# Zero rows in the memory cell's small products, and an early operation on ScalarE

## The chip, the cores and the metric

One core of a Trainium2 chip runs the whole program in one launch. The metric is the device time of that launch in microseconds (us). The time before is 1978.71 us, the median of three runs (1972.72 to 1982.28). A span in the profile is the stretch from the first to the last recorded instruction of one profiled execution.

## The reference, cut to what matters

The program is two transformer blocks over 256 tokens of width 1024, in fp32: feed-forward layers, gated linear attention, stick-breaking attention, and then a second block with a state-space branch (S5), a matrix-memory cell (mLSTM) beside it, and a layer that gathers experts from a table. The change lies in the memory cell and in one line of the set-up. The cell has 4 heads, and 16 learned tokens stand before the 256 (272 positions). The reference computes it in chunks with a carried state:

```python
w_intra = jnp.exp(d_log - m_t[..., None])
s = jnp.einsum('bhtd,bhsd->bhts', q, k) * w_intra
num = jnp.einsum('bhts,bhsd->bhtd', s, v) + ...   # the carried state's part
den = jnp.sum(s, axis=-1) + ...
h = num / jnp.maximum(jnp.abs(den), jnp.exp(-m_t))[..., None]
```

The kernel computes the same over all 272 positions at once. Position s weighs on token t by exp(c(s) + mm(t)), where c is the input gate less the running sum of the forget gates, and mm is minus the running maximum of c.

## The kernel before, in words

The framework plans the order of the instructions of each engine from the program text: every instruction has the priority of its place in the text, each engine takes what is ready, and tiles of a tag share a fixed number of buffers (tag "t2" has 12). Once planned, each engine runs its list in order. So a line further down can be run before one further up.

Block two (`block2`, line 1083) projects the tokens, runs `mlstm` (line 930), then the gates and output projections. Inside `mlstm`:

- `convolve` and `maps` make q, k and v. Positions are cut in three (`STILES`): 16, 128 and 128. The values of the first 16 go to `v0`, two tiles of 16 x 512 (lines 934 and 972).
- `s5_scan` (line 822, called at line 980) is traced inside this function: 67 steps of five small operations on GpSimd (POOL), lines 842 to 846, one chain from first to last. It comes ahead of the gates in the text.
- Lines 984 to 1007 make the gates: `c`, its running maximum `M`, `mm` (4 x 2 x 256, a row for each head), `cc` (c transposed into columns, line 1005) and `sel`, a table of ones by which a product over 4 rows spreads the row of one head over 128 partitions. `sel` comes by a DMA on SyncE's queue (SP), line 1007.
- `first(h)` (line 1010): the exponents `bp` (line 1013 in bf16; line 1015 over 4 rows), the exps on ScalarE (lines 1017 to 1020), the scores of k and q (line 1025; the first position tile has 16 columns of weights, so its result has 16 rows), and a product over 4 rows for the floor of the denominator (line 1026).
- `second(h)` (line 1033): the gate z by three-part split products (lines 171 to 173, tile `ip`), then denominator and numerator: `weigh` adds a product over 16 rows (line 1044) and two over 128 rows (lines 1045 and 1046).
- `third(h)` (line 1061): the norm of the head and the split for the next projection.

The split products (lines 171 to 173) run on operands in fp32r, one pass each; those of the cell run in fp32, and each shows as two instructions in the trace ("x2"). Weights come as raw tiles of 1 MB by SP's queue (line 153), and ScalarE (line 186) and VectorE (line 187) split them.

At the start (`Net.__init__`, line 34, and `run`, line 1384) VectorE fills some constants, SP's queue loads x and the first weights, and ScalarE's first work is line 191 on x.

Of the kernel before, what the change touches and what calls it, by code (L numbers as in the profile page):

```python
# [7 lines left out]
F32 = mybir.dt.float32  # L8
# [4 lines left out]
AF = mybir.ActivationFunctionType  # L13
OP = mybir.AluOpType
# [3 lines left out]
T = 256  # L18
NF = 22
NM = 16  # L20
# [5 lines left out]
STILES = ((0, 16), (16, 128), (144, 128))  # L26
# [6 lines left out]
class Net:  # L33
    def __init__(self, ctx, tc, a):
        self.tc, self.nc, self.a, self.ctx = tc, tc.nc, a, ctx
        nc = self.nc
        self.const = ctx.enter_context(tc.tile_pool(name="const", bufs=1))
        self.keep = ctx.enter_context(tc.tile_pool(name="keep", bufs=1))
        self.dense = ExitStack()
        self.act = self.dense.enter_context(tc.tile_pool(name="act", bufs=1))  # L40
        self.tmp = self.dense.enter_context(tc.tile_pool(name="tmp", bufs=2))
        self.weighed = ExitStack()
        self.wp = self.weighed.enter_context(tc.tile_pool(name="wp", bufs=3, side="right"))
        self.dram = ctx.enter_context(tc.tile_pool(name="dram", bufs=1, space=bass.MemoryType.DRAM))
        self.ps = ctx.enter_context(tc.tile_pool(name="ps", bufs=1, space=PSUM))
        self.latest, self.since, self.early = (), 0, {}
        self.wbufs = 2, 4
        c = self.const
        self.vecs = c.tile([128, a["vecs"].shape[1]], F32, name="vecs")
        nc.sync.dma_start(self.vecs, a["vecs"])  # L50
        self.eps = c.tile([128, 1], F32, name="eps")
        nc.vector.memset(self.eps, 1e-6)
        self.eps2 = c.tile([128, 1], F32, name="eps2")
        nc.vector.memset(self.eps2, 1e-12)
        self.ones = c.tile([128, 128], F32, name="ones")
        nc.vector.memset(self.ones, 1.0 / D)

# [872 lines left out]
    def mlstm(self, st, u4):  # L930
        nc, a = self.nc, self.a
        xc, q, k = self.slots(TL, "xc"), self.slots(T, "mq"), self.slots(TL, "mk")
        gp = self.ps.tile([36, TL], F32, tag="ms", name="gp")
        v0 = [self.t2([16, 512], "mv0") for _ in range(2)]
        v = [self.slot([128, 2, 512], "mv") for _ in range(2)]
        va = lambda i, o: (v0[o // 512][:, o % 512:o % 512 + 128] if i == 0 else
                           v[o // 512][:, i - 1, o % 512:o % 512 + 128])
# [16 lines left out]
        def maps(b, x_m):  # L954

            for j in range(2):
                n, xm = 2 * b + j, x_m[:, j, :]
                bd = self.t2([128, 3, 128], "bd")
                nc.sync.dma_start(bd, a["ml_bd"][n])
                nc.tensor.matmul(gp, self.gw[:, n, 0, :], xc(n), start=n == 0, stop=False)  # L960
                nc.tensor.matmul(gp, self.gw[:, n, 1, :], xm, start=False, stop=n == 7)
                ps = self.bank([128, T], name="mqp")
                nc.tensor.matmul(ps, bd[:, 0, :], xc(n)[:, NM:], start=True, stop=True)
                nc.scalar.activation(q(n), ps, AF.Copy)
                ps = self.bank([128, TL], name="mkp")
                nc.tensor.matmul(ps, bd[:, 1, :], xc(n), start=True, stop=True)
                nc.scalar.activation(k(n), ps, AF.Copy)
                ps = self.bank([128, 3, 128], name="mvp")
                for i, (o, r) in enumerate(STILES):
                    nc.tensor.matmul(ps[0:r, i, :], xm[:, o:o + r], bd[:, 2, :], start=True, stop=True)  # L970
                c = slice(n % 4 * 128, n % 4 * 128 + 128)
                nc.vector.tensor_copy(v0[n // 4][:, c], ps[0:16, 0, :])
                nc.vector.tensor_copy(v[n // 4][:, :, c], ps[:, 1:3, :])

        x_m = {}
# [17 lines left out]
        F, c, M, one = (self.t2([4, TL], n) for n in ("F", "c", "M", "one"))  # L993
# [1 line left out]
        nc.vector.memset(one, 1.0)  # L995
        nc.vector.scalar_tensor_tensor(c, gp[0:4], self.V("ml_b_if")[0:4], F, op0=OP.add, op1=OP.subtract)
        nc.vector.tensor_tensor_scan(M, one, c, 0.0, OP.mult, OP.max)
        mm = self.t2([4, 2, T], "mm")
        nc.vector.tensor_scalar(mm[:, 0], M[:, NM:], -1.0, None, op0=OP.mult)
        nc.vector.tensor_tensor(mm[:, 1], mm[:, 0], F[:, NM:], OP.subtract)  # L1000
        ps = self.bank([128, 3, 4], name="cc")
        cc = self.t2([128, 3, 4], "cc")
        for i, (o, r) in enumerate(STILES):
            nc.tensor.transpose(ps[0:r, i, :], c[:, o:o + r], self.ident[0:4, 0:4])
            nc.vector.tensor_copy(cc[0:r, i, :], ps[0:r, i, :])
        sel = self.t2([4, 4, 128], "sel")
        nc.sync.dma_start(sel, a["sel"])
        y = self.pair(T, "my")

        def first(h):  # L1010

            bp = self.bank([128, 512], name="bp")
            nc.tensor.matmul(bp, self.identb, self.later, start=True, stop=False)
            for i in range(2):
                nc.tensor.matmul(bp[:, 256 * i:256 * i + 256], sel[:, h, :], mm[:, 0, :], start=False, stop=i == 1)
            w0, w = self.t2([16, T], "w0"), self.t2([128, 384], "w")
            nc.scalar.activation(w0, bp[0:16, 0:256], AF.Exp, bias=cc[0:16, 0, h:h + 1])
            nc.scalar.activation(w[:, 0:128], bp[:, 256:384], AF.Exp, bias=cc[:, 1, h:h + 1])
            nc.scalar.activation(w[:, 128:256], bp[:, 128:256], AF.Exp, bias=cc[:, 1, h:h + 1])
            nc.scalar.activation(w[:, 256:384], bp[:, 384:512], AF.Exp, bias=cc[:, 2, h:h + 1])  # L1020
            s1 = self.bank([128, 384], name="ms1")
            s0 = self.bank([128, 2, T], name="ms0")
            for dst, ks, t0 in ((s0[0:16, 0, :], slice(0, 16), 0), (s1[:, 0:256], slice(16, 144), 0), (s1[:, 256:384], slice(144, 272), 128)):
                for d in range(2):
                    nc.tensor.matmul(dst, k(2 * h + d)[:, ks], q(2 * h + d)[:, t0:], start=d == 0, stop=d == 1)
            nc.tensor.matmul(s0[:, 1, :], sel[:, h, :], mm[:, 1, :], start=True, stop=True)
            em = self.t2([128, T], "em")
            nc.vector.scalar_tensor_tensor(w0, s0[0:16, 0, :], 1.0 / 16, w0, op0=OP.mult, op1=OP.mult)
            nc.scalar.activation(em, s0[:, 1, :], AF.Exp)
            nc.vector.scalar_tensor_tensor(w, s1, 1.0 / 16, w, op0=OP.mult, op1=OP.mult)  # L1030
            return w0, w, em

        def second(h, w0, w, em):
            wt = self.weights("w_in", 6 + h)
            zp = self.accum([128, 2, T], "ip")
            for j in range(2):
                self.acc(zp[:, j, :], wt, j, lambda kk: [t[:, NM:] for t in st.x(kk)])
            z = self.aux([128, 2, T], "mz")
            nc.vector.tensor_tensor(z, zp, st.f[:, NM:].unsqueeze(1).to_broadcast([128, 2, T]), OP.mult)
            nc.scalar.activation(z, z, AF.Sigmoid)  # L1040
            num, den = self.bank([128, 2, T], name="num"), self.bank([128, T], name="den")

            def weigh(dst, l):
                nc.tensor.matmul(dst, l(0), w0, start=True, stop=False)
                nc.tensor.matmul(dst, l(1), w[:, 0:256], start=False, stop=False)
                nc.tensor.matmul(dst[:, 128:256], l(2), w[:, 256:384], start=False, stop=True)

            weigh(den, lambda i: self.onesf[0:STILES[i][1], :])
            for d in range(2):
                o = h * 256 + d * 128  # L1050
                weigh(num[:, d, :], lambda i: va(i, o))
            dn = self.t2([128, T], "dn")
            nc.scalar.activation(dn, den, AF.Abs)
            nc.vector.tensor_tensor(dn, dn, em, OP.max)

            nc.scalar.activation(dn, dn, AF.Square, scale=1e-3)
            hh = self.t2([128, 2, T], "hh")
            nc.vector.tensor_tensor(hh, num, z, OP.mult)
            return hh, dn
# [366 lines left out]
def cols(v):  # L1426
    return v.reshape(-1, 128).T
# [10 lines left out]
def layouts(d):  # L1438

    f = np.float32  # L1440
    a, where, parts, at = {}, {}, [], 0
    bias = np.zeros(128, f)
# [4 lines left out]
    for n, v in named + [("ml_b_if", bias)]:  # L1447
        c = cols(v)
# [9 lines left out]
    w = d["gla_w_in"]  # L1458
# [4 lines left out]
    t = np.arange(128)  # L1463
# [15 lines left out]
    c = [g[n][0].reshape(16, 2, 16, 64).transpose(1, 3, 0, 2).reshape(128, 16, 16) for n in ("ssm_c_re", "ssm_c_im")]  # L1479
# [6 lines left out]
    wif, w = np.zeros((24, 128, 36), f), g["ml_w_if"][0].reshape(24, 128, 8)  # L1486
    wif[:, :, 0:4], wif[:, :, 32:36] = w[:, :, 0:4], w[:, :, 4:8]
    a["ml_wif"] = wif.transpose(1, 0, 2)
    a["sel"] = np.repeat(np.eye(4, dtype=f)[:, :, None], 128, 2)
    a["ml_out"] = wblocks(g["w_ml_out"], 8, 256)  # L1490
    a["w_out"] = wblocks(g["w_out"], 8, 256)
    a["peer_q"] = wblocks(g["peer_w_q"], 8, 256)
# [20 lines left out]
```

## Time and profile before

| | before |
|---|---|
| median of three runs | 1978.71 us (1972.72 to 1982.28) |
| the profiled execution, its own time | 1977.11 us |
| its span | 1975.3 us |
| mean granted clock of TensorE | 0.986 of full |
| TensorE (PE) busy | 1791.1 us (91%) |
| VectorE (DVE) busy | 1351.8 us (68%) |
| ScalarE (ACT) busy | 853.6 us (43%) |
| GpSimd (POOL) busy | 656.1 us (33%) |

The page gives busy times of the engines, their course in 40 slices, the DMA queues, and the chain of work that ended last. That chain lies 57% on PE and 29% on DMA. The memory cell lies between some 1060 and 1186 us of the span; from about 1330 us on the gathers of the expert layer fill the DMA engines.

### The profile page before, as it was taken

Reading aid. Unit: us, or ns where it says so; the run is one execution under the profiler, and the core shown is the slowest. Engines: PE = TensorE matmul, PEld = TensorE weight load, DVE = VectorE, ACT = ScalarE, POOL = GpSimd, SP = SyncE. Lnnn points to the kernel's source line nnn. Section 1 sums busy time; section 2 is a strip of 40 time slices with the busy share of each in tenths; the row PEclk is TensorE's granted clock in tenths of the full one; section 3 lists DMA queues with packets and bytes.
Section 4 is the critical chain, followed back from the end, with each engine's and each line's share of the span. In section 5 each row is a group of like instructions: output and inputs, shape, how many; then the busy total and the mean of one; then the engine's idle time right before and its main releaser. Section 6 shows DMA issues by size and latency. Waiting matters only on the chain.

```text
span 1975.3 us, 31529 instructions
## 1 busy us (share of the span) xinstructions
PE 1791.1 (91%) x12113; PEld 1445.5 (73%) x12113; DVE 1351.8 (68%) x2498; ACT 853.6 (43%) x1394; POOL 656.1 (33%) x834
## 2 busy tenths in 40 slices
PE   7999899999999999999999998988777778778776
PEld 7999899999999998899998688973333433334222
DVE  6765677975676666675677376787767676777755
ACT  5544635544544456554444466452222222322223
POOL 5001312041250100200144871245445454554552
PEclk9999999999999999999999999999999999999999
DMA  5556424555645553364465224589999999999996
GB/s 206 194 177 202 164 86 172 201 190 179 211 172 164 191 189 125 107 224 159 169 204 164 77 79 159 191 332 419 420 420 419 420 419 420 419 420 419 420 420 268
DMA packets 81310, 493.31 MB, mean 250 GB/s; under 512 B 14420, under 2 KB 16724, under 8 KB 28936
## 3 DMA queue, kind: packets, MB, share of 16 engines
q0 software_dynamic: 37152, 268.45, 32.8%
q1 hardware_dynamic: 36472, 219.53, 31.7%
q10 hardware_dynamic: 7536, 3.31, 0.8%
q8 instruction: 96, 1.57, 0.3%
q14 instruction: 54, 0.44, 0.1%
HBM read 488.80 MB, written 2.13 MB: 249 GB/s over the span
## 4 chain that ended last, share of the span: by engine, by line
PE 57%; DMA 29%; DVE 6%; issue 3%; ACT 3%; POOL 2%; SPq 0%; POOLq 0%; ACTq 0%; DVEq 0%
DMA uv<-in_peer_uv,route 26%; PE o L171 4%; PE o L172 4%; PE o L173 4%; PE up L172 4%; PE up L173 4%; PE gate L171 4%; PE up L171 4%; PE gate L173 4%; PE gate L172 4%; PE acc L1361 2%; DVE wlo L187 2%; PE ip L173 1%; PE ip L171 1%; PE ip L172 1%
## 5 line engine op out<-in xcount | busy, mean ns | idle before, releaser
L187 DVE TENSOR_TENSOR wlo<-raw,whi 128x1024 fp32r<-128x1024 f32 (+3 forms) x451 | 515.6, 1159 | 189.0 <-ACT whi L186 178.7
L1361 PE MATMUL acc<-uv,dg 128*128 128x512 f32 x1016 | 479.8, 620 | 137.4 <-ACT dg L1359 137.4
L186 ACT ACTIVATE whi<-raw 128x1024 fp32r<-128x1024 f32 (+3 forms) x451 | 424.9, 963 | 360.5 <-PE gate L172 76.7
L1361 PEld LDWEIGHTS acc<-uv,dg 128*128 128x128 f32 x1016 | 189.6, 195 | 421.8 <-ACT dg L1359 223.5
L1313 POOL DMA_INDIRECT uv<-in_peer_uv,route x254 | 325.4, 1281 | 325.4 <-DMA uv<-in_peer_uv,route 206.2
L1341 DVE SCALAR_TENSOR_TENSOR uv<-uv,xn 128x1024 f32<-128x1024 f32 x256 | 313.3, 1224 | 155.9 <-DMA uv<-in_peer_uv,route 149.5
L171 PE MATMUL gate<-xp,whi 128*128 128x256 f32 x704 | 198.8, 282 | 7.6 <-ACT whi L186 7.6
L173 PE MATMUL gate<-xp,wlo 128*128 128x256 f32 x704 | 197.7, 281 | 4.3 <-DVE wlo L187 4.3
L1349 ACT ACTIVATE route<-route 128x2 f32<-128x2 f32 x129 | 26.2, 203 | 402.0 <-DVE uv L1341 401.9
L172 PE MATMUL gate<-xp,whi 128*128 128x256 f32 x704 | 197.3, 280 | 0.0
L173 PE MATMUL o<-hh,wlo 128*128 128x256 f32 x704 | 194.9, 277 | 0.1
L171 PE MATMUL o<-hh,whi 128*128 128x256 f32 x704 | 194.8, 277 | 0.0
L172 PE MATMUL o<-hl,whi 128*128 128x256 f32 x704 | 194.8, 277 | 0.0
L173 PE MATMUL up<-xp,wlo 128*128 128x256 f32 x704 | 194.6, 276 | 0.0
L171 PE MATMUL up<-xp,whi 128*128 128x256 f32 x704 | 194.5, 276 | 0.0
L172 PE MATMUL up<-xp,whi 128*128 128x256 f32 x704 | 194.5, 276 | 0.0
L171 PEld LDWEIGHTS gate<-xp,whi 128*128 128x128 f32 x704 | 134.9, 192 | 8.6 <-ACT whi L186 7.9
L173 PEld LDWEIGHTS gate<-xp,wlo 128*128 128x128 f32 x704 | 134.5, 191 | 5.6 <-DVE wlo L187 5.6
L172 PEld LDWEIGHTS gate<-xp,whi 128*128 128x128 f32 x704 | 134.8, 191 | 0.4 <-DVE xp L192 0.2
L217 POOL TENSOR_TENSOR sumsq<-x 128x256 f32<-128x256 f32 x9 | 7.0, 780 | 381.4 <-DVE x L306 203.8
L173 PEld LDWEIGHTS o<-hh,wlo 128*128 128x128 f32 x704 | 132.6, 188 | 0.2 <-DVE wlo L187 0.2
L171 PEld LDWEIGHTS up<-xp,whi 128*128 128x128 f32 x704 | 132.3, 188 | 0.0
(459 smaller groups left out, 3860.2 us busy)
## 6 DMA issues: line engine op xcount, KB each, us to landing
raw<-in_ffn_w_up SPq DMA_DIRECT2D x44, 1024.0 KB, 4.8
raw<-in_ffn_w_down SPq DMA_DIRECT2D x64, 704.0 KB, 4.2
raw<-in_ffn_w_gate SPq DMA_DIRECT2D x43, 1024.0 KB, 4.8
raw<-in_w_in SPq DMA_DIRECT2D x18, 1024.0 KB, 4.9
raw<-in_gla_in SPq DMA_DIRECT2D x12, 1024.0 KB, 4.8
raw<-in_sb_in SPq DMA_DIRECT2D x12, 1024.0 KB, 4.8
raw<-in_peer_q SPq DMA_DIRECT2D x8, 1024.0 KB, 7.2
raw<-in_gla_w_out SPq DMA_DIRECT2D x4, 1024.0 KB, 4.8
```

The lines of the kernel that those rows point to most:

```text
L171: nc.tensor.matmul(ps, hi, xh, start=start and n == 0, stop=False)
L172: nc.tensor.matmul(ps, hi, xl, start=False, stop=False)
L173: nc.tensor.matmul(ps, lo, xh, start=False, stop=stop and n == len(steps) - 1)
L186: return (self.nc.scalar.activation(h, src, AF.Copy).ins, self.nc.vector.tensor_tensor(l, src, h.bitcast(F32), OP.subtract).ins)
L187: self.nc.vector.tensor_tensor(l, src, h.bitcast(F32), OP.subtract).ins)
L217: g.tensor_tensor(q, src, src, OP.mult)
L1313: nc.gpsimd.indirect_dma_start(out=out, out_offset=None, in_=table, in_offset=bass.IndirectOffsetOnAxis(ap=ids, axis=0))
L1341: lastdot = nc.vector.scalar_tensor_tensor(u, u, 1.0, xn[i], op0=OP.mult, op1=OP.mult, accum_out=dots[:, k:k + 1]).ins
L1349: gelu = nc.scalar.activation(w[:, ks], dots[:, ks], AF.Gelu_apprx_tanh).ins
L1361: lastv = nc.tensor.matmul(acc[i][b], dg, vt[:, b * 512:(b + 1) * 512], start=False, stop=hd == 7 and k == 14).ins
```

## The change

1. A tile `pair` of 128 x 2 replaces `eps2`; its first column is the old constant, and ScalarE copies the constant `eps` into the second column, ahead of all other ScalarE work in the text. Nothing reads that column.
2. `v0`, `mm`, `sel` and `w0` grow from 16 or 4 rows to 128. `v0` (2 tiles of 128 x 512) and `mm` (128 x 512) are filled with zeros on GpSimd first, `cc[:, 0, :]` with -1e30 on GpSimd, and `sel` comes with 124 rows of zeros from the host (256 KB for 8 KB).
3. The products over 4 rows (lines 1015, 1026) and over 16 rows (line 1044) go over 128 rows. The scores of the first position tile (line 1025) take 128 columns of k for 16, so that 128 rows come out; the exp and the scaling of `w0` go over 128 partitions, and the bias of -1e30 makes the added rows zero.

```diff
-        self.eps2 = c.tile([128, 1], F32, name="eps2")
-        nc.vector.memset(self.eps2, 1e-12)
+        pair = c.tile([128, 2], F32, name="eps2")
+        self.eps2 = pair[:, 0:1]
+        nc.vector.memset(pair, 1e-12)
+
+        nc.scalar.activation(pair[:, 1:2], self.eps, AF.Copy)
...
-        v0 = [self.t2([16, 512], "mv0") for _ in range(2)]
+
+        v0 = [self.t2([128, 512], "mv0") for _ in range(2)]
+        for t in v0:
+            nc.gpsimd.memset(t, 0.0)
...
-                nc.vector.tensor_copy(v0[n // 4][:, c], ps[0:16, 0, :])
+                nc.vector.tensor_copy(v0[n // 4][0:16, c], ps[0:16, 0, :])
...
-        mm = self.t2([4, 2, T], "mm")
-        nc.vector.tensor_scalar(mm[:, 0], M[:, NM:], -1.0, None, op0=OP.mult)
-        nc.vector.tensor_tensor(mm[:, 1], mm[:, 0], F[:, NM:], OP.subtract)
+        mm = self.t2([128, 2, T], "mm")
+        nc.gpsimd.memset(mm, 0.0)
+        nc.vector.tensor_scalar(mm[0:4, 0], M[:, NM:], -1.0, None, op0=OP.mult)
+        nc.vector.tensor_tensor(mm[0:4, 1], mm[0:4, 0], F[:, NM:], OP.subtract)
         ps = self.bank([128, 3, 4], name="cc")
         cc = self.t2([128, 3, 4], "cc")
+        nc.gpsimd.memset(cc[:, 0, :], -1e30)
...
-        sel = self.t2([4, 4, 128], "sel")
+        sel = self.t2([128, 4, 128], "sel")
...
-            w0, w = self.t2([16, T], "w0"), self.t2([128, 384], "w")
-            nc.scalar.activation(w0, bp[0:16, 0:256], AF.Exp, bias=cc[0:16, 0, h:h + 1])
+            w0, w = self.t2([128, T], "w0"), self.t2([128, 384], "w")
+            nc.scalar.activation(w0, bp[:, 0:256], AF.Exp, bias=cc[:, 0, h:h + 1])
...
-            for dst, ks, t0 in ((s0[0:16, 0, :], slice(0, 16), 0), (s1[:, 0:256], slice(16, 144), 0), (s1[:, 256:384], slice(144, 272), 128)):
+            for dst, ks, t0 in ((s0[:, 0, :], slice(0, 128), 0), (s1[:, 0:256], slice(16, 144), 0), (s1[:, 256:384], slice(144, 272), 128)):
...
-            nc.vector.scalar_tensor_tensor(w0, s0[0:16, 0, :], 1.0 / 16, w0, op0=OP.mult, op1=OP.mult)
+            nc.vector.scalar_tensor_tensor(w0, s0[:, 0, :], 1.0 / 16, w0, op0=OP.mult, op1=OP.mult)
...
-            weigh(den, lambda i: self.onesf[0:STILES[i][1], :])
+            weigh(den, lambda i: self.onesf)
...
-    a["sel"] = np.repeat(np.eye(4, dtype=f)[:, :, None], 128, 2)
+    a["sel"] = np.repeat(np.eye(128, 4, dtype=f)[:, :, None], 128, 2)
```

## Rows read from the trace of the kernel before

**Rows 1.** The page, busy time, share of the span and instructions of each engine.

```profile
PE 1791.1 (91%) x12113; PEld 1445.5 (73%) x12113; DVE 1351.8 (68%) x2498; ACT 853.6 (43%) x1394; POOL 656.1 (33%) x834
```

**Rows 2.** Busy time by stretches: length, engines' busy us (instructions), PEclk, DMA share, GB/s.

```profile
1103.50:1105.50 2.00, 0.20 (x2) 0.03 (x1) 1.92 (x5) 1.40 (x2) 1.76 (x7) 1.00 0.00 0
1105.90:1109.30 3.40, 3.40 (x9) 1.68 (x9) 2.50 (x6) 0.63 (x1) 3.24 (x6) 0.52 0.10 19
...
1116.00:1119.40 3.40, 3.40 (x18) 2.65 (x17) 0.35 (x2) 2.08 (x4) 3.01 (x15) 1.00 0.00 0
1119.40:1122.80 3.40, 3.40 (x15) 3.04 (x13) 1.59 (x4) 3.37 (x9) 2.93 (x15) 0.50 0.01 2
...
1127.30:1143.00 15.70, 15.70 (x75) 10.38 (x73) 6.71 (x11) 6.13 (x13) 13.91 (x59) 1.00 0.18 67
```

**Rows 3.** The chain that ended last, 1126 to 1143 us: start, us, what.

```profile
1131.22 0.62 PE ms L1026 x2
1131.84 0.43 PE den L1044 x2
1132.28 0.63 PE den L1045 x2
...
1139.85 2.47 PE ms L1025 x12
```

**Rows 4.** The same chain, 1104 to 1123 us.

```profile
1116.19 1.06 PE bp L1015 x4
1117.24 0.43 PE ms L1026 x2
```

**Rows 5.** Line 1025: weight loads, count, ns min/median/max, first and last start, forms.

```profile
L1025 PEld LDWEIGHTS ms<-mq,mk x48: 92/190/338, 1106.0 to 1141.9; 128*128 128x128 f32 x32, 128*16 128x16 f32 x16
```

**Rows 6.** Stretches as in Rows 2, at the gate maps (lines 925 to 927).

```profile
907.80:914.60 6.80, 6.80 (x33) 6.80 (x33) 2.19 (x3) 0.00 (x0) 0.00 (x0) 0.50 0.01 2
```

**Rows 7.** Lines 1017 and 1053 on ScalarE: ns min/median/max, starts, forms.

```profile
L1017 ACT ACTIVATE w<-bp,cc x4: 450/458/466, 1118.6 to 1143.0; 16x256 f32<-16x256 f32 x4
L1053 ACT ACTIVATE dn<-den x4: 365/378/384, 1124.7 to 1159.4; 128x256 f32<-128x256 f32 x4
```

**Rows 8.** Groups by form on POOL: count, busy us, mean ns, idle before.

```profile
L377 POOL MEMSET s<- 128x512 f32 x1 | 0.5, 526 | 0.0
```

**Rows 9.** Timeline of POOL, 1031 to 1034 us: start, us, engine, line.

```profile
1031.66 0.61 POOL L220 TENSOR_TENSOR sq<-x 128x256 f32<-128x256 f32 x1 [0.23 <-DVE x L595]
1032.21 0.20 POOL L604 MEMSET tiny<- 128x128 f32 x1
1032.38 1.71 POOL L221 TENSOR_TENSOR sumsq<-sumsq,sq 128x256 f32<-128x256 f32 x1
```

**Rows 10.** Timeline of POOL, a step of the scan beside VectorE, and its last operation.

```profile
1105.63 2.18 POOL L842 TENSOR_TENSOR s5t<-V,s5a 128x32 f32<-128x32 f32 x1
...
1172.25 0.25 POOL L846 TENSOR_TENSOR V<-V,s5t 128x32 f32<-128x32 f32 x1
```

**Rows 11.** Timeline of VectorE, 1103 to 1121 us.

```profile
1107.63 0.33 DVE L999 TENSOR_SCALAR mm<-M 4x256 f32<-4x256 f32 x1
...
1107.99 0.41 DVE L1000 TENSOR_TENSOR mm<-mm,F 4x256 f32<-4x256 f32 x1
```

**Rows 12.** DMA issues: line's tile, queue, count, KB each, median us to landing.

```profile
raw<-in_w_in SPq DMA_DIRECT2D x18, 1024.0 KB, 4.9
```

**Rows 13.** Timeline of SP's queue, 1000 to 1170 us.

```profile
1108.11 0.38 SPq L1007 DMA_DIRECT2D sel<-in_sel  x1
```

**Rows 14.** Timeline of ScalarE, its first instruction.

```profile
4.85 1.28 ACT L191 ACT_TABLE_LOAD   x1 [4.85 <-DMA x<-in_x]
```

**Rows 15.** The chain that ended last, 0 to 22 us.

```profile
2.12 5.96 DMA x<-in_x
8.10 0.91 ACT xp L191 x2
```

**Rows 16.** The same chain, 1168 to 1226 us.

```profile
1183.71 4.10 ACT vc L855 x4
```

## The prediction

> **What bounds the kernel now.** I read the page first: TensorE (PE) is busy for 91% of the span [rows 1], so an edit that takes PE time out of a stage in which PE never idles should shorten the span, and an edit on another engine should not, unless it makes PE wait. Then the stretches: around the memory cell PE is busy for the whole of 1105.9 to 1143 us, but not all of that is work at full clock. The granted clock reads 0.52 in 1105.9 to 1109.3 and 0.50 in 1119.4 to 1122.8 (the 1.2 GHz level of the two, 1.2 and 2.4), and 1.00 in the other stretches [rows 2]. The reader should look at what went before each fall: before the first PE did 0.20 us of work in 2.00 us, before the second it was busy for all of 3.40 us, but 12 of its 18 instructions there were products over 4 rows (six of them in [rows 4]). Then the chain of waits: in the cell it runs through PE, piece after piece, and each piece has a length that can be compared with its like [rows 3, 4].
>
> **Part 1, products go over 128 rows.** The same two instructions over 256 columns take 0.43 us when the pair before them also ran on few rows (line 1026 after line 1015, both over 4 rows [rows 4]; line 1044, over 16, after line 1026, over 4 [rows 3]), and 0.62 to 0.63 us when the rows change between 128 and few (line 1026 after line 1025, line 1045 after line 1044 [rows 3]). So a change of shape costs 0.19 to 0.20 us, not the small product itself. The chain has 23 such pieces between 1123 and 1162 us that stand behind another fp32 product of the cell: 21 in `weigh` (den and num of lines 1044 and 1045) and two of line 1026. 23 x 0.195 = 4.5 us. Line 1025 takes 2.47 us for 12 instructions [rows 3], twice; eight at half of 0.43 and four over 128 columns at half of that again (my estimate) come to 2.15, so 0.3 us each is left for its own change from 16 to 128 columns of weights, 0.6 in all. Together 5.1 us. Changes between fp32 and the fp32r or bf16 products beside them stay, and I count nothing for them.
>
> What it adds on PE: 16 weight loads grow from 16 columns to 128, from 92 to 190 ns [rows 5]. If nothing hid them, that is 16 x 0.098 = 1.6 us; one instruction over 256 columns takes 0.215 us (half of 0.43), which is longer than the load, so I take 0 and keep 1.6 for the range.
>
> The clock: 3.4 us at 0.50 with PE busy throughout hold 1.7 us of work at full clock. I take 1.7 back, since the padded products fill all rows for 256 columns, as most of 1127.3 to 1143 does at clock 1.00 [rows 2]. It is not certain: the clock also read 0.50 for 6.8 us at the gate maps, whose products do use 128 rows but only 36 columns [rows 6], so the number of rows is not all that counts. The lower bound is 0. The first slow stretch follows an idle PE, which nothing here fills: 0, with 1.7 as the other bound.
>
> A rule of the Trainium skill speaks against this part. The row said that pairs over few rows take the same 0.43 us as a pair over 128 would, and that only the change costs. The page "TensorE: Matmul & The Clock Gate", section "Why this matters for your kernels", says that a single product over K=32 takes the same time as over K=128, and the trace agrees as far as the pair itself goes. By that rule alone, zeros would buy nothing on PE, and the sum would be that of the neutral rival below; the 0.19 us of the change of shape stands in the rows and not in the rule.
>
> **Part 2, the wider work on other engines.** The exp and the scaling of `w0` go over 128 partitions: 16 x 256 takes 458 ns on ScalarE and 128 x 256 takes 378 [rows 7], so 0. `sel` becomes 256 KB. 1024 KB land in 4.9 us [rows 12], so about 1.2 us by proportion; it is issued at 1108.11 [rows 13], and even with a whole 1 MB load ahead of it, it lands near 1114.2, before its first reader at 1116.19 [rows 4]. So 0.
>
> **Part 3, zeros on GpSimd.** A fill of 128 x 512 takes 0.53 us [rows 8]; there are three, and a small one for `cc`. All four share POOL's queue with the scan. The scan ends at 1172.5 [rows 10], and its reader on the chain, the copies `vc`, starts at 1183.71 [rows 16]: 11 us of cover, of which my gain takes 6.8 and the fills 1.7. So the longer scan costs 0. The fill of `mm` is the delicate one. The first writer of `mm` on VectorE (line 999) now waits for it; behind line 999 on VectorE stand the copies of `cc`, and PE's transposes for `cc` wait for those. In the trace `mm` is complete at 1108.40 [rows 11] and first used at 1116.19, 7.8 us later. A POOL operation beside VectorE's work took 2.18 us where its like takes 0.25 [rows 10], so the fill can come some microseconds late. Bounds: 0 and 5 us (two such hold-ups and the fill), and I take 1.0, nearer to the lower end, since most of the delay falls in the 7.8 us.
>
> Whether the plan puts the fill inside the scan at all is seen from another fill: `tiny` ran between line 220 and the line 221 that depends on it, although its place in the text is further down [rows 9]. So a free operation slips into such a chain. I take it that this one does too.
>
> **Part 4, the early copy on ScalarE.** The table load takes 1.28 us from 4.85 on, when the first x landed [rows 14]. With a constant to work on it runs before that. But the chain at the start goes through another landing of x at 8.10 and the ScalarE work behind that [rows 15], after all that the load held up. I take 0; bounds 0 and a gain of 1.3. A loss is excluded by the 4 us in which ScalarE has nothing else.
>
> **The sum.** -5.1 (shapes) -1.7 (clock) +1.0 (the fill) = -5.8 us. Against the profiled execution, 1977.11 us, that is 1971.3. The median of the runs is 1.6 us above that execution, so 1972.9 us against the median, 0.3% less. It passes to the end: PE is busy for all 15.70 us of 1127.3 to 1143 [rows 2], the splits and weight loads behind that wait for products or buffers that PE gives, and the scan alone does not move along, with the cover told above.
>
> **The rivals.**
> - Neutral: the zeros buy nothing, as the rule has it, or the next wait takes the gain back: a new plan of the queues can put another load or split late. For it: every list is planned anew, and the fill adds a wait. Against it: PE is full here and the 0.19 us shows in every pair. About 1979.7 (0 gain, 1.0 for the fill). Chance 0.20.
> - More: the first slow stretch goes as well and the table load counts in full: -5.1 -1.7 -1.7 -1.3 = -9.8, 1968.9. For it: both are in the rows; against it: the idle PE before 1105.5 and the landing at 8.10. Chance 0.13.
> - Slower: the fill of `mm` lands behind the whole scan in POOL's list. Then `mm` is complete at 1172.5 + 0.53 + 0.77 = 1173.8 and line 1015 starts 57.6 us late. Other projections can be taken ahead until their buffers run out; I take half, +29, near 2008. It decides from a fill that ends after 1115.4 (1116.19 less 0.77): from there each us late is a us of PE. Against it stands `tiny`. Chance 0.12.
> - The zeros remove the stalls but not the slow stretch (the change does half of what it is for): 1974.6, within the forecast.
>
> **How the numbers follow.** The forecast, 1972.9, has 0.55, with a range of its own of 1968 to 1980 from the bounds (-9.8; -5.1 + 1.6 + 5 = +1.5). The medians themselves spread by some 5 us either way. The range 1964 to 1984 takes in the neutral rival and the larger gain, and leaves out the slower one and the tails. A difference of 0.5%, 9.9 us, is about what a measurement here can tell from none. Faster by more needs the larger gain or the upper edge of the forecast: 0.13. Slower by more is the third rival: 0.12. Within it: 0.75.
>
> **What would show it right or wrong.** In the trace after: pairs of lines 1026, 1044 and 1045 at 0.43 us in the chain, line 1025 near 2.2; clock 1.00 in the stretch after the products of line 1015; the fill of `mm` between operations of the scan near 1105; line 999 within 3 us of line 997; the table load done before 4.85, and the first split product of the kernel no earlier than about 1 us. Wrong would be pairs still at 0.62, PE idle before line 1004 or 1015, or a fill at the scan's end.

## The result and the profile after

The changed kernel takes 2024.53 us (median of four runs, 2023.48 to 2029.93); the kernel before, run beside it, takes 1980.49. The ratio is 1.0227, with a 95% interval of 1.0202 to 1.0252: slower by 44 us, where I had forecast 1972.9 and a range to 1984. The third rival, told there with a chance of 0.12, is what happened, at one and a half times its price.

The page of the kernel after, first the busy times, then the 40 slices for PE and its clock. Lines of the code stand a few lower than before: the split products are now 174 to 176, the scan 845 to 849, the fill of `mm` 1005 and that of `cc` 1010, the transposes 1012, the copies of `cc` 1013, the products of `mm` 1023 and 1034, the scores 1033, `weigh` 1052 to 1054.

```profile
PE 1781.5 (88%) x12113; PEld 1447.4 (72%) x12113; DVE 1348.7 (67%) x2498; ACT 853.6 (42%) x1394; POOL 652.9 (32%) x838
...
PE   8999899999999999999998099988777788788776
...
PEclk9999999999999999999999599999999999999999
```

PE is busy for 9.6 us less than before [rows 1], so there is less work in it, as forecast. But slice 23 reads 0, and the clock reads 5 there. A whole slice of 50 us in which PE does next to nothing is new. The stretches around it (columns as in [rows 2]):

```profile
1100.00:1110.00 10.00, 5.03 (x34) 4.23 (x33) 4.42 (x8) 2.64 (x3) 9.06 (x33) 1.00 0.00 0
1110.00:1120.00 10.00, 0.00 (x0) 0.00 (x0) 0.00 (x0) 0.00 (x0) 8.69 (x41) 0.51 0.00 1
1120.00:1160.00 40.00, 0.00 (x0) 0.00 (x0) 0.00 (x0) 0.00 (x0) 34.90 (x164) 0.50 0.00 0
1160.00:1170.00 10.00, 8.41 (x38) 7.05 (x39) 2.58 (x9) 3.94 (x10) 1.07 (x5) 0.76 0.00 0
```

From 1110 to 1160 us only POOL works, the fifth engine in the row. PE, VectorE, ScalarE and the DMA engines stand still together, so they all wait for something on POOL. The timelines name it: VectorE, then POOL, then PE (start, us, engine, line, operation; in brackets the idle time before and what ended it).

```profile
1105.53 0.73 DVE L1003 TENSOR_TENSOR_SCAN M<-one,c 4x272 f32<-4x272 f32 x1
1161.14 0.28 DVE L1006 TENSOR_SCALAR mm<-M 4x256 f32<-4x256 f32 x1 [54.88 <-POOL cc L1010]
1161.35 0.14 DVE L1013 COPY cc<-cc 16x4 f32<-16x4 f32 x1
```

```profile
1160.39 0.25 POOL L849 TENSOR_TENSOR V<-V,s5t 128x32 f32<-128x32 f32 x1
1160.58 0.52 POOL L1005 MEMSET mm<- 128x512 f32 x1
1161.04 0.10 POOL L1010 MEMSET cc<- 128x4 f32 x1
```

```profile
1104.93 1.89 PE L1033 MATMUL ms<-mq,mk 128*128 128x256 f32 x8
1161.55 0.27 PE L1012 MATMUL cc<-ident,c 4*128 4x4 f32 x1 [54.72 <-DVE cc L1013]
```

Both fills stand behind the last operation of the scan. VectorE's first write of `mm` waits 54.88 us for them; behind it on VectorE stands the first copy of `cc`, and PE's second transpose waits for that copy: 54.72 us, with nothing of PE's list run ahead.

The other part of the forecast is in the trace as well. The chain that ended last, in the cell after the wait (start, us, what):

```profile
1174.42 0.86 PE bp L1023 x4
1175.29 2.17 PE ms L1033 x12
1177.46 0.43 PE ms L1034 x2
...
1183.59 0.43 PE den L1052 x2
1184.02 0.43 PE den L1053 x2
```

The pairs that took 0.62 and 0.63 [rows 3] take 0.43, the scores 2.17 (I had worked out 2.15; 2.47 before), the products of line 1015 are 0.86 for 1.06 [rows 4]. So the change does what it says, and a wait of its own making takes five times as much.

### The profile page after: what moved, and what is told of

Its sections match the earlier page's. It is cut to its first block, busy times and chain, and to the rows that moved or that the text cites. A ratio compares the mean times of both kernels' runs of the same rounds, so it can differ in the third digit from the quotient of the medians.

```text
span 2023.2 us, 31527 instructions
## 1 busy us (share of the span) xinstructions
PE 1781.5 (88%) x12113; PEld 1447.4 (72%) x12113; DVE 1348.7 (67%) x2498; ACT 853.6 (42%) x1394; POOL 652.9 (32%) x838
## 4 chain that ended last, share of the span: by engine, by line
PE 53%; DMA 29%; DVE 6%; POOL 6%; issue 3%; ACT 3%; SPq 0%; POOLq 0%; ACTq 0%; DVEq 0%
DMA uv<-in_peer_uv,route 27%; PE o L174 4%; PE o L175 4%; PE o L176 4%; PE up L175 4%; PE gate L174 4%; PE up L174 4%; PE up L176 4%; PE gate L176 4%; PE gate L175 4%; DVE wlo L190 2%; PE ip L174 1%; PE ip L176 1%; PE ip L175 1%; ACT whi L189 1%
## 5 line engine op out<-in xcount | busy, mean ns | idle before, releaser
L1321 POOL DMA_INDIRECT uv<-in_peer_uv,route x254 | 330.2, 1300 | 319.9 <-DMA uv<-in_peer_uv,route 202.8
L175 PEld LDWEIGHTS o<-hl,whi 128*128 128x128 f32 x704 | 132.8, 189 | 0.0
```

Of the source, the lines that this page charges most:

```text
L175: nc.tensor.matmul(ps, hi, xl, start=False, stop=False)
L1321: nc.gpsimd.indirect_dma_start(out=out, out_offset=None, in_=table, in_offset=bass.IndirectOffsetOnAxis(ap=ids, axis=0))
```

## The experiments

My theory after these rows: the place of the two fills in POOL's list is all of the loss. What it leaves open is why the plan put them there, whether the gain really reaches the end once they are out of the way, and which part of the change makes it.

**1. The fills on VectorE.** Line numbers are those of the kernel after; the rest is unchanged.

```diff
-        nc.gpsimd.memset(mm, 0.0)
+        nc.vector.memset(mm, 0.0)
...
-        nc.gpsimd.memset(cc[:, 0, :], -1e30)
+        nc.vector.memset(cc[:, 0, :], -1e30)
```

> As the changed kernel, but VectorE writes the zeros of mm and the -1e30 of cc, not GpSimd. Theory (the two fills stood behind the whole scan in GpSimd's list, and that alone cost the time): PE's idle stretch of 1110 to 1160 us is gone, cc's first transpose lies near 1109, and the time is that of the kernel before less 5.1 (shapes), 1.7 (clock) and about 1.0 (PE did 0.97 us more in the first 50 us of the changed kernel's trace): about 1973, 0.996 of the kernel before. Rival (the wider products, loads or VectorE and ScalarE work also cost time that the idle stretch hid): the idle stretch is gone but the time is 1981 or more. Rival (the scan itself became the bound, whoever fills): PE still waits near 1110 for tens of us, above 2010.

Measured: 1976.26 us, ratio 1.0003 (0.9986 to 1.002) to the kernel before. The 50 us are gone, but so is the gain: the ratio is not the 0.996 of the theory, the time is some 5 us short of the 1981 of the first rival, and the reason is one that I had not named. PE's waits between 1100 and 1200 us (what waited, what for: us, times, longest):

```profile
PE ip L174 <- DVE mix L908: 8.5, 1, 8.5
PE cc L1012 <- DVE c L1002: 1.8, 1, 1.8
PE ms L1033 <- ACT w L1028: 1.4, 1, 1.4
PE sy L868 <- ACT vc L858: 0.9, 1, 0.9
```

The second of them was there before as well. The first is new, and it lies behind the cell. Followed back through the timelines of PE, VectorE and POOL:

```profile
1174.51 0.55 PE L174 MATMUL ip<-xp,whi 128*128 128x256 f32 x1 [8.46 <-DVE mix L908]
```

```profile
1171.38 0.69 DVE L1076 SCALAR_TENSOR_TENSOR hh<-hh,vecs,sx 128x256 f32<-128x256 f32 x1 [5.42 <-POOL sx L1075]
1172.29 1.47 DVE L1076 SCALAR_TENSOR_TENSOR hh<-hh,vecs,sx 128x256 f32<-128x256 f32 x1 [0.21 <-POOL sx L1075]
1173.68 0.68 DVE L908 TENSOR_TENSOR mix<-ip,f 128x512 f32<-128x512 f32 x1
```

```profile
1170.18 0.25 POOL L849 TENSOR_TENSOR V<-V,s5t 128x32 f32<-128x32 f32 x1
1170.42 0.94 POOL L1075 TENSOR_SCALAR sx<-xc,vecs 128x256 f32<-128x256 f32 x1
```

For head 3, and for it alone, the skip product `sx` is given to GpSimd (`third`, line 1067 before, 1075 here). It stands behind the scan, VectorE's `hh` waits for it, `mix` stands behind `hh` on VectorE, and PE needs the accumulator that `mix` reads. Before, the scan's last operation started at 1172.25 [rows 10], GpSimd was through with `sx` at 1174.33, and VectorE came to that `hh` at 1177.03, so nobody waited. Now the last product of the cell ends at 1152.0 for 1162.3, and the scan ends only 2 us sooner. The shorter cell had made the end of the scan the next bound, 8.46 us of it. The granted clock adds to it: it reads 0.50 in the first 3 us of work behind the wait (columns as in [rows 2]), which holds 1.5 us less work than at full clock.

```profile
1174.50:1177.50 3.00, 2.99 (x14) 3.00 (x15) 3.00 (x3) 2.38 (x3) 1.27 (x1) 0.50 0.00 0
```

8.46 and 1.5 are 10 us, as much as the gain that experiments 5 and 11 show.

**2. The fills ahead of the scan.** The tiles are taken and filled on GpSimd next to `v0`, at the head of `mlstm`.

```diff
         for t in v0:
             nc.gpsimd.memset(t, 0.0)
+        mm = self.t2([128, 2, T], "mm")
+        nc.gpsimd.memset(mm, 0.0)
+        cc = self.t2([128, 3, 4], "cc")
+        nc.gpsimd.memset(cc[:, 0, :], -1e30)
```

> As the changed kernel, but the tiles mm and cc are taken and filled on GpSimd at the head of the memory cell, next to the fills of v0, so that the fills stand ahead of the scan in GpSimd's list. Theory (the place in the list costs the time, not the engine): both fills run near 1036 us, no idle stretch, and the time is within 2 us of the kernel with VectorE's fills, about 1973. Rival (GpSimd is the wrong engine for them wherever they stand, as it disturbs VectorE): 5 us or more above that kernel. Rival (two of the 12 buffers of that kind are held some 70 us longer, and the loads of bd wait for buffers): gaps on PE between 1040 and 1105 and 1978 or more.

Measured: 1977.04 us, ratio 0.9996 (0.9984 to 1.0009); the fill of `mm` runs at 1037.04, ahead of the scan, and PE's wait for `mix` is 9.7 us. It is within 2 us of experiment 1, as forecast, though neither comes to 1973. So it is the place in the list and not the engine, and the second wait stands here too.

**3. and 4. The small fill by itself.** In both, VectorE fills `mm`. In the first the fill of `cc` on GpSimd goes to a tile with storage of its own (`self.const.tile`), in the second it stays in a shared buffer as in the kernel after. The text of the fill stands at the same place.

> As the kernel with VectorE's fill of mm, with cc filled on GpSimd at the same place in the text as in the changed kernel, but in a tile with storage of its own instead of one of the 12 shared buffers. Theory A (the fill is planned late because its shared buffer comes free only when the scan already runs): the fill of cc runs in the first 50 us, the time is near 1973. Theory B (it is planned late because its text stands behind the scan's): the fill runs after the scan's end near 1160, and the time is that of the changed kernel within some us, 2015 to 2026.

> As the changed kernel, but VectorE writes the zeros of mm; the small fill of cc (4 columns, 101 ns in the trace of the changed kernel) stays on GpSimd in a shared buffer. Theory (the wait is for the place in the list, so the size of the fill does not count): the fill runs after the scan's end near 1160, cc's copies wait, and the time is 2015 to 2026. Rival (only mm's fill is on the path; cc's can be late since PE has the products of mm to do meanwhile): under 1990.

Measured: 2017.85 and 2030.3 us in single runs. The fill of `cc` in the two traces (ns min/median/max, first and last start), in the order told:

```profile
L1010 POOL MEMSET cc<- x1: 101/101/101, 24.7 to 24.7; 128x4 f32 x1
```

```profile
L1010 POOL MEMSET cc<- x1: 101/101/101, 1165.8 to 1165.8; 128x4 f32 x1
```

In the second, PE waits 52.2 us for the copy of `cc`: 101 ns of fill cost as much as both fills did, so the size does not count. Its time is 4.3 us above the range that I gave; of the 5.8 us that it has over the kernel after, 5.2 lie ahead of the cell (the first product of `mqp` starts at 1071.09 for 1065.85), where the edit does nothing.

In the first the fill runs at 24.7 us, as theory A has it, no such wait exists, and PE waits 5.7 us, for `myh`, behind the cell. The time, 2017.85, would fit theory B, and can't be set beside the others: the products of the feed-forward layers, which no edit here touches, take 283 ns on the mean for 276 in experiment 1, in stretches whose granted clock is the same (1.00 in 300 to 600 us of both). Of the 44.5 us that its span has over that of experiment 1, 42.4 lie ahead of the first product of `mqp`. Why they were slower in this run, no run shows. From the first product of `mqp` to the first that reads `vc`, where the edit works, it takes 124.4 us and experiment 1 takes 125.1; the second of the pair takes 174.1, the kernel after 173.7.

**5. Skip product on VectorE.** Experiment 1 with the second wait removed too.

```diff
-                (nc.gpsimd if h == 3 else nc.vector).tensor_scalar(sx, xc(n)[:, NM:], self.V("ml_skip", n), None, op0=OP.mult)
+                nc.vector.tensor_scalar(sx, xc(n)[:, NM:], self.V("ml_skip", n), None, op0=OP.mult)
```

> As the kernel whose fills of mm and cc are on VectorE, and the skip product sx of head 3 (line 1075) goes to VectorE too, where heads 0 to 2 have it. Theory (the gain of the cell, 8 to 10 us, is there, and was lost to a new wait: PE idle for 8.46 us at 1166.05 to 1174.51, for VectorE's mix, which stood behind head 3's hh, which waited 5.42 us for GpSimd's sx behind the scan): that idle stretch falls below 2 us and the time is 1968 to 1971, 0.995 to 0.9965 of the kernel before. Rival (the end of the scan holds PE up by another way too, the copies vc or GpSimd's products of myl): the idle stretch moves to the next of these, and the time stays within 2 us of the kernel before.

Measured: 1968.26 us, ratio 0.9949 (0.9931 to 0.9966). PE's waits between 1095 and 1200 us:

```profile
PE cc L1012 <- DVE c L1002: 1.8, 1, 1.8
PE ms L1033 <- ACT w L1028: 1.4, 1, 1.4
PE ip L174 <- DVE mix L908: 0.8, 1, 0.8
```

8.5 us have become 0.8, and the time is 10 us below that of the kernel before (1977.42 beside it), as the theory has it. The gain was there and had been lost to the second wait.

**6. The kernel before with that edit alone.** The control.

> The kernel before with nothing but sx of head 3 on VectorE. Theory (in the kernel before PE is busy in 1120 to 1180, and the wait for GpSimd's sx is hidden; it shows only when the cell gets shorter): no difference, ratio 0.999 to 1.001. Rival (the wait counts already, so the gain of the version with all edits comes from this edit and not from the zeros): 0.996 or less.

Measured: 1976.91 us, ratio 0.9996 (0.9976 to 1.0016). As the theory has it: where the cell is long, the wait is hidden and its removal is worth nothing. The zeros with their fills mended gain nothing by themselves (1.0003), nor does this edit (0.9996); both together gain 0.5%.

**7. The wait without the zeros.** The kernel before with one line more.

```diff
         mm = self.t2([4, 2, T], "mm")
+        nc.gpsimd.memset(mm, 0.0)
```

> The kernel before with one instruction more: GpSimd fills mm (4 rows) at the same place in the text as in the changed kernel. Nothing is padded. Theory (the place of the fill alone makes the loss): the fill runs behind the scan, PE idles for some 50 to 58 us ahead of cc's transposes, and the time is 2022 to 2036, as much above the changed kernel's as the zeros gain, 5 to 10 us. Rival (the wider work has part in the loss): below 2010.

Measured: 2037.52 us in a single run. The fill of 0.51 us starts at 1165.89, behind the scan, and PE waits:

```profile
PE cc L1005 <- DVE cc L1006: 51.7, 1, 51.7
PE cc L1005 <- DVE c L996: 1.8, 1, 1.8
```

One instruction costs 60 us, and none of the wider work has a part in it. That is 1.5 us above the range that I gave, and 13 us above the changed kernel, where I had expected 5 to 10. Of the 60, 51.7 are the wait; most of the rest is PE's clock behind it, told below.

**8. The early copy by itself.** The kernel before with item 1 of the change.

> The kernel before with the early copy on ScalarE alone. Theory (PE starts sooner, as in the changed kernel's trace: first product at 6.11 us and not 7.63): PE's work in the first 50 us is 0.9 to 1.1 us more than the 39.57 of the kernel before, the time 1 us less, which a single run can't show. Rival (the gain in the first 10 us is lost at the next landing of weights): 39.4 to 39.8 us of work in the first 50.

Measured: 1977.88 us in a single run. The first 50 us of the kernel before and of this one (columns as in [rows 2]):

```profile
0.00:50.00 50.00, 39.57 (x297) 38.11 (x298) 34.49 (x44) 27.35 (x37) 25.03 (x34) 1.00 0.59 209
```

```profile
0.00:50.00 50.00, 40.54 (x304) 39.02 (x305) 35.27 (x45) 27.93 (x38) 24.87 (x34) 1.00 0.59 212
```

PE gets 0.97 us more done, as in the kernel after, whose first product starts at 6.11 us for 7.63 before. Whether that microsecond reaches the end, no total here can show.

**9. and 10. The two halves of the zeros.** Both start from the kernel before with `sx` of head 3 on VectorE. The first pads only the products of `mm`, with VectorE's fill; the second only what was 16 wide, `cc` filled by VectorE.

> The kernel before with sx of head 3 on VectorE, and of the padding only the products of mm (lines 1015 and 1026, 4 rows to 128; VectorE fills mm). w0 and the products over 16 rows stay. Theory (the loss is 0.19 us at each change between few and 128 rows, so what counts is how many changes go): the 24 products of den and num over 16 rows keep their mean pitch of 0.30 to 0.31 us, the 24 of mm fall to 0.15 to 0.23, and the cell gains a fourth or less of what all the zeros gain, 1 to 2 us: ratio to the kernel before 0.998 to 1.000. Rival (the products over 4 rows pay most, as they hold TensorE's clock at 0.50): two thirds of the gain or more is here, ratio 0.997 or less, and the cell's stretch of clock 0.50 is gone, which the other half keeps.

> The kernel before with sx of head 3 on VectorE, and of the padding only what was 16 wide: v0, w0, cc, the first products of line 1025 and those of den and num. The products of mm stay over 4 rows. Theory: the 24 products of den and num fall from 0.30 to about 0.18 us of pitch, the 48 of line 1025 from 0.24 to 0.18; three fourths or more of the gain of all the zeros is here, 4.5 to 6.5 us: ratio 0.9965 to 0.998. Rival (clock, as above): the ratio is 0.9985 or more and PE's clock still reads 0.50 for some microseconds in the products over 4 rows.

Measured: 1975.55 us, ratio 0.9972 (0.9953 to 0.9991), and 1972.89 us, 0.9962 (0.9946 to 0.9978). The second lies just beyond the theory's range of 0.9965 to 0.998, on the side of more gain, the first between the theory and the rival, and the intervals overlap, so the totals can't split the gain. The granted clock goes as the rival has it, 1.00 in the cell of the first and 0.70 in 1116 to 1120 of the second, but a cell without zeros can read 1.00 too (experiment 6), so that does not decide. The pitches could be read: in the first the 24 products of `den` and `num` over 16 rows stay at 0.31 us from one start to the next, and the 24 of `mm` fall to 0.21; in the second all 72 of `den` and `num` come to 0.18, while the 24 of `mm` over 4 rows rise from 0.25 to 0.33. A wait of 1.4 us and the slow stretch lie among those 24; whether their neighbours over 128 rows have a part in the rise is not shown.

**11. Both waits mended, no fill on VectorE's chain.** Experiment 2 with `sx` on VectorE.

> The changed kernel with the fills of mm and cc on GpSimd ahead of the scan in the text, and sx of head 3 on VectorE: the version with both waits mended, and no fill on VectorE's chain from c to mm (0.54 us there when VectorE fills). Theory (both waits are all that stood in the way): 0.9935 to 0.9965 of the kernel before, as the version whose fills are on VectorE (0.9949), at most 1 us apart. Rival (a shared buffer held from the head of the cell on, or the fills on GpSimd, cost something that the first wait hid): 0.998 or more.

Measured: 1970.35 us, ratio 0.9946 (0.9928 to 0.9965). It is the same as experiment 5 within what can be told, as the theory has it, and both are faster than the two kernels of this case.

**12. Taken ahead, filled late.** Experiment 11, but only the tiles are taken at the head of the cell; the text of the two fills stands where the changed kernel has it.

> The kernel with the fills ahead of the scan and sx of head 3 on VectorE (0.9946), but only the tiles mm and cc are taken at the head of the cell; their two fills on GpSimd stand at the changed kernel's place in the text, behind the scan's. The buffers are those that were free near 1036 us where the fills stood ahead. Theory A (a fill loses to the scan by its place in the text once the scan can run, however early its buffer is free): the fills run behind the scan, PE waits for cc some 50 us, and the time is 2015 to 2035. Theory B (the buffer's release alone decides): the fills run before the scan's first step and the time is 1966 to 1976.

Measured: 2026.08 us in a single run, in the range of theory A. PE waits 54.7 us for the copy of `cc`. POOL's timeline around the start of the scan, and the two fills as groups (count, busy us, mean ns):

```profile
1037.73 0.98 POOL L940 MEMSET mv<- 128x512 f32 x2
1068.47 0.22 POOL L847 TENSOR_TENSOR s5t<-V,s5a 128x16 f32<-128x16 f32 x1 [29.76 <-DVE V L837]
```

```profile
L1006 POOL MEMSET mm<- 128x512 f32 x1 | 0.5, 524 | 0.0
L1010 POOL MEMSET cc<- 128x4 f32 x1 | 0.1, 101 | 0.0
```

POOL stood idle for 29.76 us ahead of the scan, and the fills still run at 1164.4 and 1164.8. Yet this does not rule out theory B, because the edit did not do what I meant it to do. In experiment 11 the trace has the fills wait for no other engine. Here, as in the kernel after, the fill of `mm` waits for two counters: the one on which the third `bd` load of `maps` lands (read from the order of the loads), and PE's. The fill of `cc` waits for that of the fourth load, and for PE's. So taking the tiles further up in the text reserved no buffers: both fills again got buffers that had held `bd` tiles. PE's last reading of the third:

```profile
1079.92 1.03 PE L978 MATMUL mvp<-bd,xm 128*16 128x128 f32 x6
```

It ends at 1080.95, and the scan had begun at 1068.47. So the late place has two causes. The buffer comes free only when the scan already runs; experiment 3, where the storage has no earlier user, shows the fill long before. From then on the scan's operations, which stand further up in the text, go first, for 83 us, up to the last. A fill whose text stands ahead of the scan, but whose buffer comes free during it, is not among the experiments, so what the place in the text costs by itself is not shown.

## Why the prediction was wrong, point by point

**The step that failed** is the end of Part 3: "So a free operation slips into such a chain. I take it that this one does too." `tiny` did run between lines 220 and 221 [rows 9], but the fill is not free as `tiny` is. In the traces `tiny` waits for no other engine; the fill of `mm` waits until PE has left its buffer, at 1077.2 in the kernel after, and the scan had begun at 1064.69. From there on one of the scan's operations, of a higher priority than the fill, is ready whenever POOL comes free; in 1110 to 1160 us POOL is idle for about 0.1 us at a time, between two operations that depend on each other. The fill runs at 1160.58, behind the last of them. With storage of its own it runs at 24.7 us (experiment 3), with its text ahead of the scan, and a free buffer, at 1037.04 (experiment 2); its size does not count (experiment 4). Why the plan let `tiny` in between two operations of one chain, and no fill between two of the scan's, no run shows.

**The price of that rival** failed as well. I took half of 57.6 us as hidden by other projections "taken ahead until their buffers run out". Nothing was: PE did 0.00 us of work in 1110 to 1160. The transposes of `cc` stand in PE's list, and the list runs in order; I had said in Part 3 that they wait, and then priced the rival as if the rest of PE could pass them. That the wait, 54.72 us, comes near the late start of 57.6 is in part luck: PE stopped at the transposes of `cc` and not only at line 1015, which makes it longer, and `mm` was complete at 1161.86 (1161.45 + 0.41) and not at 1173.8, the scan ending 12 us sooner with VectorE idle beside it. With nothing hidden, the rival would have read 57.6 less a gain of some 6 to 10: about 50 us, against the 44 measured.

**The cover of 11 us** in Part 3 was the third error, hidden by the first. I looked for the scan's reader on the chain and found `vc` [rows 16]. I did not list what else stands behind the scan in POOL's list. `sx` of head 3 does, and its reader had a slack of only 2.7 us (`sx` done at 1174.33, read at 1177.03). The gain is larger than that slack, so mending the fills alone leads to the wait and the slow stretch of experiment 1, and brings nothing. A list of what a stage hides has to be read in the other direction too: what the stage runs into when it gets shorter.

**The shapes** were right in mechanism and nearly in size. The table gives the sum of the distances from one start to the next of the cell's own products, from the first of `bp` over `mm` to the last of `num`, without the split products between them, in us: the kernel before, experiment 6 (same products, clock 1.00 throughout) and experiment 11 (all zeros).

| products | before | experiment 6 | experiment 11 | the fall: forecast, measured |
|---|---|---|---|---|
| `den` and `num`, 72 | 16.97 | 16.97 | 12.78 | 4.1 (21 pieces), 4.2 |
| scores, 32 of the 48 | 7.56 | 6.38 | 5.75 | 0.6, 0.6 from experiment 6 on |
| over `mm`, 24 | 6.05 | 6.05 | 4.83 | 0.4, 1.2 |
| norm and bf16 products, 10 | 2.26 | 2.26 | 2.18 | 0, 0.1 |
| sum | 32.85 | 31.67 | 25.54 | 5.1, 6.1 from experiment 6 on |

What I left out is line 1015, whose four instructions fell from 1.06 [rows 4] to 0.86 us on three of the four heads (on the second they took 0.86 before too, behind a product over 4 rows [rows 4]): the change between it and the bf16 or split product ahead of it went too, though I had said that such changes stay. The split products are not in the table; where they meet the cell's own products they take some 0.4 us more in experiment 11 than in experiment 6, so that of the 6.1 us about 5.8 are left. The wider weight loads cost nothing, as taken: line 1033 with 12 loads of 128 columns takes 2.17 us. The rule of the Trainium skill that I weighed ("TensorE: Matmul & The Clock Gate", section "Why this matters for your kernels": a single product over K=32 takes as long as over K=128) holds for the product itself, 0.43 us for the pair at either width, and does not tell of the neighbours; by it the cell's sum would have stayed at 31.67, and the measurement decides for 25.54.

**The clock** term of 1.7 us was half right. The slow stretch that it counts, at the products over `mm` on 4 rows, shows in the kernel before and in experiment 10 (0.70 in 1116 to 1120), and not in experiments 6 and 8, whose products there are those of the kernel before; experiment 8 has one at 1108 to 1112, ahead of them. In the cells whose products over `mm` have zeros, and that have no long wait (experiments 1, 5, 9 and 11), the clock reads 1.00. So 1.2 (the scores of the table, before and in experiment 6) to 1.7 us was to be had, but not in each execution: it is a chance, not a term.

**The fill of `mm`**, where it is done in time, costs less than the 1.0 us taken: on VectorE it and `cc`'s take 0.54 us of the chain from `c` to `mm` (experiment 1), ahead of the scan nothing that the total shows (experiment 11).

**The early copy** I put at 0, because the chain at the start goes through a landing of x at 8.10 [rows 15]. That landing came sooner too (ScalarE takes it at 7.20 in the kernel after), and PE gained 0.97 us, inside my bound of 1.3.

**The sum that would have been right**, had nothing waited: 5.8 for the shapes, 1.2 for the clock and 1.0 for the copy, which no total shows by itself, are 8.0 us, against 10.1 (6.7 to 13.6) measured in experiment 5 and 10.7 (6.9 to 14.3) in experiment 11. In the changed kernel the same gain is seen from the other side: PE waits 54.7 us, and the time is 44.0 longer, which leaves 10.7, roughly, since a slow stretch and a wait of 2.3 us for `mix` follow there.

## What to carry to other kernels

A free instruction is free only by its place in the list of its engine: before an engine is given one more operation, look at when its buffer comes free, at what stands ahead of it there, and whether that chain ever waits for another engine. Where the chain did not, nothing got in here; storage of its own, another engine, or an earlier place in the text with a buffer that was free took the wait away. Then look at everything that stands behind the long chain, not only at its reader on the critical path, because a stage that gets shorter meets those next. And where an edit "gains nothing", look for a wait that appeared at the far end of the stage before giving up the mechanism.

## What the runs showed of the hardware

**After a pause PE's clock came back later where the products ran over few rows.** Two kernels pause for over 50 us in the same place and then run the same cell, the one after over 128 rows, experiment 7 over 4 and 16. Stretches of 2 us (busy us, instructions, granted clock, DMA share, GB/s), first the kernel after, whose PE starts again at 1161.55, then experiment 7, whose PE starts again in the first stretch shown:

```profile
1162.00:1164.00 2.00, 2.00 (x8) 0.50 0.00 0
1164.00:1166.00 2.00, 2.00 (x9) 0.78 0.00 0
1166.00:1168.00 2.00, 1.96 (x9) 1.00 0.00 0
```

```profile
1166.00:1168.00 2.00, 1.15 (x5) 0.50 0.00 0
1168.00:1170.00 2.00, 2.00 (x6) 0.50 0.00 0
...
1176.00:1178.00 2.00, 2.00 (x8) 0.50 0.00 0
1178.00:1180.00 2.00, 2.00 (x9) 0.75 0.04 8
```

PE is busy throughout in both. In the kernel after the clock is back at 2.4 GHz by 1166; in experiment 7 it stays at 1.2 GHz to beyond 1178, with five more stretches of full busy time at half speed. Two more kernels with zeros and a pause, experiments 4 and 12, lie nearer to the kernel after: PE starts again at 1166.16 and 1165.32, and the clock reads 1.00 from 1172 on. Only one of the four kernels ran over few rows, once, and why its clock stays down is not shown. At half speed the 12 us or so of experiment 7 hold about half as much work, which is most of what its loss of 60 us has beyond the wait of 51.7.

**GpSimd is faster when VectorE is still.** Between 1110 and 1160 us the scan's operations on 128 x 32 take 250 ns on the mean in the kernel after, where VectorE is idle, and 288 to 316 in the kernel before, where it works; 41 steps go into the 50 us for 35, and the scan ends 12 us sooner. PE, ScalarE and the DMA engines are idle in that window too, but it is VectorE that counts: in the kernel before, 159 of the scan's 335 operations have no VectorE operation beside them, PE is busy beside every one of these, and none takes over 256 ns. Nor does every VectorE operation count: seven steps beside a split of line 187 alone take 1.19 us at the median, and 22 beside the reciprocals of line 451 at most 0.26. The Trainium skill ("SBUF — State Buffer", section "A bandwidth-pool intuition that's wrong (but worth ruling out)") says that of GpSimd and a VectorE operation on two ports one blocks the other wholly. The long steps, of 2.18 us for 0.25 at most [rows 10], agree with that; which VectorE operations use two ports, no trace shows.
